# First SwiGLU: the loads of the first wide group's weight sums are put behind the first narrow group's evictions

## The chip, the cores and the metric

The kernel runs on one core of a Trainium2 chip. The metric is the device time of one execution in microseconds (us). The core has five instruction queues that are told of here: PE (TensorE, with PEld for its weight loads), DVE (VectorE), ACT (ScalarE), POOL (GpSimd) and SP (SyncE, which issues DMAs only). DMAs issued by SP appear in the profile as queue q1, those issued by POOL as queue q0.

## The reference, cut to what matters

Two layers, each with a SwiGLU of half weight, a token mixer of three branches, and a second SwiGLU. The sequence has 256 tokens, the model width is 1024, the inner width of a SwiGLU 2816, and all is in float32.

```
def swiglu_ffn(h, w_in, w_out):
    gate, up = jnp.split(h @ w_in, 2, axis=-1)
    return (jax.nn.silu(gate) * up) @ w_out

for l in range(DEPTH):
    x = x + FFN_RESID * swiglu_ffn(rms_norm(x, ffn1_norm[l]), ffn1_w_in[l], ffn1_w_out[l])
    ...                                      # the mixer
    x = x + FFN_RESID * swiglu_ffn(rms_norm(x, ffn2_norm[l]), ffn2_w_in[l], ffn2_w_out[l])
```

## The kernel before, in words

All weights lie in one stream in HBM, cut into chunks of 128 x 1024 float32 (512 KB). A chunk is loaded by SP into one of five `raw` buffers (`load`, line 145). ACT then copies it into `whi` in the matmul's reduced format (line 172), and DVE writes the remainder into `wlo` (line 173); there are four buffers of each. A product of full precision is made of three matmuls, with the high and low parts of the activations and weights (`mm3x`, lines 218 to 220). `units` is the list of chunks in the order of use, `next_sub` hands out the next split chunk, and splits are made three units ahead (`AHEAD`). The split of a unit comes with high priority. The instructions of each engine stand in an order that the framework's scheduler chooses from a simulated timeline, so an instruction whose operands are free can stand earlier in its queue than in the source.

The first product of a SwiGLU, `h @ w_in`, is done in two ways. Seven narrow groups of 256 gate and 256 up columns are done plainly: four chunks each, 48 matmuls, into two PSUM banks (`ps_in`). When a narrow group's fourth chunk is done (c == 3), ACT makes `s`, the SiLU of the gates (line 511), and DVE multiplies it by the up half into `at` (line 513), for each half b of the tokens. These are the evictions of the group; both need `rs_x`, the reciprocal norm of each token, which POOL computes (line 298) from squares that ACT makes of `x` (line 348).

Two wide groups of 512 columns are done with seven products of blocks in place of eight, in the manner of Strassen and Winograd: blocks b11, b12, b21, b22 of the weights, and sums t1 to t4 of them. The sums t1 = b11 + b12 and t3 = b22 + b12 are made by POOL's DMAs in `load_sums`: four plain loads (line 163), and four that add onto what lies there (line 166). t1 goes to tiles named xsum, two for each wide group, and t3 to ysum. t2 and t4 are made by DVE from these and a loaded block (lines 195 and 190). For the first wide group (j = 0) xsum lies in the buffers `vg` and `zt`, and ysum in `xbc`, which holds the transposed input x0 at the very start. For the second (j = 1) xsum lies in a buffer of its own, `big12b`, and ysum again in `xbc`, after the first group's reads.

`_ffn_order` sets the order of the units. In the first SwiGLU of the program, key (0, 0), twelve narrow units (three groups) come first, then those of the first wide group with narrow ones between: b11, two narrow, t1, one narrow, t2, one narrow, t3, one narrow, b22, one narrow, b21, one narrow, t4, one narrow, and then the second wide group in the same way. In the other SwiGLUs the sums of the first wide group are loaded before the SwiGLU begins; in the first, `load_sums(key, 0)` stands behind the first unit.

At the start SP loads, in this order: the transposed input x0 in four parts with the first chunks between them, chunks up to number 3, the input `x` by tokens (1 MB), a table `cs`, and further chunks with the mixer's `row` and `ws` among them.

Of the kernel before, what the change touches and what calls it, by code (L numbers as in the profile page):

```python
# [54 lines left out]
def _ffn_order(key):  # L55

    narrow = [("n", g, c) for g in range(NARROW) for c in range(4)]
    if key == (0, 0):
        lead, gaps = 12, [[2, 1, 1, 1, 1, 1, 1]] * 2
    else:  # L60
        lead, gaps = 4, [[2] * 7, [2, 1, 1, 2, 1, 1, 2]]
    order, narrow = narrow[:lead], narrow[lead:]
    for j in range(WIDE):
        for names, n in zip((("b11", "b12"), ("t1",), ("t2",), ("t3",), ("b22",), ("b21",), ("t4",)), gaps[j]):
            order += [(name, j, c) for name in names for c in range(2)]
            order += narrow[:n]
            narrow = narrow[n:]
    assert not narrow
    return order
# [39 lines left out]
def tile_trunk(ctx, tc, wst, xtok, xT, pos, pcol, prow, wsT, cst, out):  # L109
    nc = tc.nc  # L110
    act, dve, pool, pe = nc.scalar, nc.vector, nc.gpsimd, nc.tensor
# [22 lines left out]
    def source(i):  # L134
        return wst[starts[i] : starts[i] + P * widths[i]].rearrange("(p n) -> p n", p=P)
# [12 lines left out]

    sums = {}

    def load_sums(key, j):

        if j == 0:
            xs = [bp.tile([P, SUB_MAX], F32, name="xsum", tag=t) for t in ("vg", "zt")]
            sums[key, "y"] = bp.tile([P, 2, SUB_MAX], F32, name="ysum", tag="xbc")
        else:
            both = bp.tile([P, 2, SUB_MAX], F32, name="xsum", tag="big12b")
            xs = [both[:, c] for c in range(2)]
        for c in range(2):
            sums[key, "t1", j, c], sums[key, "t3", j, c] = xs[c], sums[key, "y"][:, c]  # L160
        for name, base in (("t1", "b11"), ("t3", "b22")):
            for c in range(2):
                pool.dma_start(out=sums[key, name, j, c], in_=source(chunk_at[key, (base, j, c)]))
        for name in ("t1", "t3"):
            for c in range(2):
                pool.dma_start(out=sums[key, name, j, c], in_=source(chunk_at[key, ("b12", j, c)]), accum_op=ALU.add)
# [37 lines left out]
    def next_sub():  # L204
        i = st["use"]
        prefetch(AHEAD + 1)
        st["use"] += 1
        return splits.pop(i)
# [7 lines left out]
    def mm3x(ps, xhi, xlo, whi, wlo, first, last, again=False):  # L216

        pe.matmul(ps, lhsT=xhi, rhs=whi, start=first, stop=False, skip_group_check=again)  # L218
        pe.matmul(ps, lhsT=xhi, rhs=wlo, start=False, stop=False, skip_group_check=again)  # L219
        pe.matmul(ps, lhsT=xlo, rhs=whi, start=False, stop=last, skip_group_check=again)  # L220
# [89 lines left out]
    def halves(b):  # L310
        return slice(P * b, P * (b + 1))
# [54 lines left out]
    def combined(nrm, n, hi, lo):  # L366

        x11, x21 = nrm.full[:, 0:4, 0:P], nrm.full[:, 0:4, P:]
        x12, x22 = nrm.full[:, 4:8, 0:P], nrm.full[:, 4:8, P:]
        if n == 0:  # L370
            o = x22
            dve.tensor_tensor(o, x22, x21, ALU.subtract)
        elif n == 1:
            o = x21
            dve.tensor_tensor(o, x11, x21, ALU.subtract)
        elif n == 2:
            o = x11
            dve.scalar_tensor_tensor(o, x22, -1.0, x11, ALU.mult, ALU.subtract)
        else:
            o = x12  # L380
            dve.scalar_tensor_tensor(o, x11, -1.0, x12, ALU.mult, ALU.subtract)
        act.copy(hi, o)
        dve.tensor_tensor(lo, o, hi.bitcast(F32), ALU.subtract)
        return hi, lo
# [10 lines left out]
    def ffn(key, nrm, nxt, last, late, aside=None):  # L395
# [14 lines left out]
        def turn_all():  # L410
            while turns:
                turn(*turns.pop(0))
# [18 lines left out]
        xs = {}  # L431
# [13 lines left out]
        def wide_step(kind, j):  # L445
            if kind == "b11":
                wide["A"] = acc.tile([P, 512], F32, name="ps_wa", tag="acc")
                product(wide["A"], plain(0, 0), True)
                wide["m"] = snap("m1", "ss")
            elif kind == "t1":  # L450
                wide["D"] = acc.tile([P, 512], F32, name="ps_wd", tag="acc")
                product(wide["D"], summed(xs[0]), True)
            elif kind == "t2":
                product(wide["A"], summed(xs[2]), False)
                wide["u"] = snap("u2", "xp")
            elif kind == "t3":
                product(wide["A"], summed(xs[1]), False)
                wide["v"] = snap("u3", "xp")
                dve.tensor_tensor(wide["v"], wide["v"], wide["D"], ALU.add)
            elif kind == "b22":  # L460
                product(wide["D"], summed(xs[3]), False)
                dve.tensor_tensor(wide["u"], wide["u"], wide["D"], ALU.add)
            elif kind == "b21":
                e = mxp.tile([P, 512], F32, name="ps_we", tag="mx")
                product(e, plain(1, 0), True)
                dve.tensor_tensor(wide["m"], wide["m"], e, ALU.add)
                gated("a0", wide["m"], 0, wide["u"])
            else:
                product(wide["A"], plain(1, 1), False)
                gated("a1", wide["A"], 1, wide["v"])  # L470
                for n in range(2):
                    s = slice(256 * n, 256 * (n + 1))
                    turns.append((2 * NARROW + 4 * j + 2 * n, [wide["u"][:, s], wide["v"][:, s]]))

        ps = None
        for n, (kind, g, c) in enumerate(_ffn_order(key)):
            if n == 8 and aside:
                aside()
            if kind != "n":
                if kind != "b12" and c == 0:  # L480
                    wide_step(kind, g)
                    if kind == "b22" and g == 0:
                        load_sums(key, 1)
                continue
            if c == 0:
                home, tag = (acc, "acc") if g % 2 == 0 else (mxp, "mx")
                ps = [home.tile([P, 512], F32, name="ps_in", tag=tag) for _ in range(2)]
            hi, lo = next_sub()
            for i in range(2):
                k, w = 2 * c + i, slice(512 * i, 512 * (i + 1))  # L490
                for b in range(2):
                    s = halves(b)
                    mm3x(ps[b], hl[:, k, 0, s], hl[:, k, 1, s], hi[:, w], lo[:, w], k == 0, k == KD - 1)
            if n == 0:
                late()
                nrm.finish()
                if key == (0, 0):
                    load_sums(key, 0)
                big = bp.tile([P, 3, 2, 4, P], F32R, name="xs", tag="big12a")
                spots = [(big[:, m, 0], big[:, m, 1]) for m in range(3)]  # L500
                spots.append([tp.tile([P, 4, P], F32R, name="xs", tag="prob") for _ in range(2)])
            elif n in (1, 2):
                for m in (0, 1) if n == 1 else (2, 3):
                    xs[m] = combined(nrm, m, *spots[m])
            turn_all()
            if c == 3:
                aa = []
                for b in range(2):
                    rcb = nrm.rc[:, b : b + 1]
                    s = tp.tile([P, 256], F32, name="s", tag="s")  # L510
                    act.activation(s, ps[b][:, 0:256], AF.Silu, scale=rcb)
                    a = at[:, g % 2, b]
                    dve.scalar_tensor_tensor(a, ps[b][:, 256:512], rcb, s, ALU.mult, ALU.mult)
                    aa.append(a)
                turns.append((2 * g, aa))
        ahl = [parts[f // 12][:, f % 12] if parts[f // 12] is not None else None for f in range(KF)]

        for h in range(2):
# [588 lines left out]
    def late(first=nrm):  # L1107
        for j in range(KD):
            first.keep(j, x0[:, j])
        for h in range(2):  # L1110
            first.squares(h)

    for l in range(DEPTH):
        params = []

        def aside(l=l, params=params):
            if l == 0:
                tables()
            params.extend(mix_params(l))
# [127 lines left out]
```

## Time and profile before

| | |
|---|---|
| median of three runs | 1264.66 us (1264.11 to 1267.06) |
| the profiled execution | 1265.76 us, span 1264.0 us |
| granted TensorE clock, mean | 0.992 |
| PE, PEld busy | 97%, 81% |
| DVE, ACT, POOL busy | 71%, 59%, 13% |
| HBM read | 253.01 MB, 201 GB/s over the span |

The span is the time from the profile's first to its last instruction, on which all times of the timeline are counted. A row of a timeline holds the start, the duration, the engine, the line of the kernel, the operation, its output and inputs, the count of merged instructions, and in square brackets the idle time before it and what ended that. A row of the chain of waits holds a start, a duration, and what the end waited for in that time. A row of a DMA queue holds packets, MB, and the time of its packets as a share of the 16 DMA engines' time in the window. A row of the stretches holds the window, its length, each engine's busy time and count, the granted clock, the DMA engines' share and GB/s. "x" loaded from in_xT is the transposed input x0.

### The profile page before, as it was taken

What the parts mean: (1) busy time and instruction counts of PE and PEld (TensorE: products, weight loads), DVE (VectorE), ACT (ScalarE), POOL (GpSimd) and SP (SyncE); (2) the same over time, 40 slices, a digit from 0 to 9 for tenths busy, and PEclk for the clock granted to TensorE, in tenths of its full rate; (3) what the DMA queues carried; (4) which work ended last, traced back from release to release, by engine and by line L of the source; (5) the groups of instructions that cost most, each with busy time, mean ns of one, the idle gap of its engine ahead of it and who ended that gap; (6) DMA issues with size and microseconds to landing.
All of it is one profiled execution on the core that took longest, in us unless ns stands there. A gap on an engine that the chain in (4) does not pass through costs nothing.

```text
span 1264.0 us, 16840 instructions
## 1 busy us (share of the span) xinstructions
PE 1221.1 (97%) x6236; PEld 1026.0 (81%) x6236; DVE 903.5 (71%) x1223; ACT 741.2 (59%) x1012; POOL 165.9 (13%) x172
## 2 busy tenths in 40 slices
PE   6899999999999899999999999999999999999998
PEld 4688888989888678778888888898888877778886
DVE  4679755897856777877568885578885566878853
ACT  5667644566576466655466664457467654756642
POOL 2100000731400010000001000054251000100000
PEclk8899999999999999999999999999999999999999
DMA  9976665544844397885549655535376456875662
GB/s 299 323 211 220 217 191 155 163 151 163 270 160 163 131 295 221 267 267 209 190 167 310 225 184 204 193 123 200 105 220 198 149 166 195 255 239 195 216 187 80
DMA packets 71651, 255.17 MB, mean 202 GB/s; under 512 B 8080, under 2 KB 8208, under 8 KB 71440
## 3 DMA queue, kind: packets, MB, share of 16 engines
q1 hardware_dynamic: 61488, 219.40, 51.1%
q0 software_dynamic: 9216, 33.56, 10.7%
q10 hardware_dynamic: 864, 1.13, 0.3%
q8 instruction: 49, 0.80, 0.3%
q14 instruction: 34, 0.28, 0.1%
HBM read 253.01 MB, written 1.05 MB: 201 GB/s over the span
## 4 chain that ended last, share of the span: by engine, by line
PE 83%; DMA 6%; DVE 6%; issue 2%; ACT 2%; POOL 1%; SPq 0%; ACTq 0%; DVEq 0%
PE ps_out L220 8%; PE ps_out L218 7%; PE ps_out L219 7%; PE ps_in L219 7%; PE ps_in L218 7%; PE ps_in L220 7%; DMA raw<-in_w 5%; PE ps_g L219 3%; PE ps_g L218 3%; PE ps_g L220 3%; DVE wlo L173 3%; PE ps_in L214 2%; PE ps_in L212 2%; PE ps_in L213 2%; PE ps_wa L219 2%; PE ps_wa L220 2%
## 5 line engine op out<-in xcount | busy, mean ns | idle before, releaser
L173 DVE TENSOR_TENSOR wlo<-raw,whi 128x1024 fp32r<-128x1024 f32 (+3 forms) x401 | 491.1, 1231 | 231.3 <-ACT whi L172 229.0
L172 ACT CAST whi<-raw 128x1024 fp32r<-128x1024 f32 (+3 forms) x401 | 414.1, 1038 | 320.3 <-PE ps_out L220 136.8
L218 PE MATMUL ps_in<-whi,xg 128*128 128x512 f32 x448 | 165.5, 402 | 16.6 <-ACT whi L172 15.5
L219 PE MATMUL ps_in<-wlo,xg 128*128 128x512 f32 x448 | 178.3, 398 | 2.7 <-DVE wlo L173 2.6
L220 PE MATMUL ps_in<-whi,xg 128*128 128x512 f32 x448 | 176.0, 397 | 0.0
L218 PEld LDWEIGHTS ps_in<-whi,xg 128*128 128x128 f32 x448 | 83.7, 191 | 35.2 <-ACT whi L172 17.2
L219 PEld LDWEIGHTS ps_in<-wlo,xg 128*128 128x128 f32 x448 | 85.6, 191 | 24.0 <-DVE wlo L173 5.8
L220 PEld LDWEIGHTS ps_in<-whi,xg 128*128 128x128 f32 x448 | 85.2, 191 | 17.3
L214 PE MATMUL ps_in<-xg,wlo 128*128 128x256 f32 x336 | 95.6, 286 | 1.5 <-DVE wlo L173 1.5
L213 PE MATMUL ps_in<-xg,whi 128*128 128x256 f32 x336 | 95.5, 286 | 0.0
L212 PE MATMUL ps_in<-xg,whi 128*128 128x256 f32 x336 | 94.5, 287 | 0.3
L219 PE MATMUL ps_g<-wlo,xg 128*128 128x512 f32 x192 | 75.8, 395 | 0.0
L219 PE MATMUL ps_out<-wlo,aa 128*128 128x512 f32 x192 | 75.7, 394 | 0.0
L220 PE MATMUL ps_out<-whi,aa 128*128 128x512 f32 x192 | 75.4, 393 | 0.0
L218 PE MATMUL ps_out<-whi,aa 128*128 128x512 f32 x192 | 75.2, 392 | 0.0
L220 PE MATMUL ps_g<-whi,xg 128*128 128x512 f32 x192 | 75.1, 391 | 0.0
L218 PE MATMUL ps_g<-whi,xg 128*128 128x512 f32 x192 | 72.8, 394 | 0.0
L214 PEld LDWEIGHTS ps_in<-xg,wlo 128*128 128x128 f32 x336 | 64.6, 192 | 1.9 <-DVE wlo L173 1.9
L213 PEld LDWEIGHTS ps_in<-xg,whi 128*128 128x128 f32 x336 | 64.7, 192 | 0.7 <-issue 0.3
L212 PEld LDWEIGHTS ps_in<-xg,whi 128*128 128x128 f32 x336 | 63.8, 192 | 1.2 <-ACT whi L172 1.0
L218 PE MATMUL ps_out<-whi,ab 128*128 128x512 f32 x160 | 62.2, 389 | 0.0
L219 PE MATMUL ps_out<-wlo,ab 128*128 128x512 f32 x160 | 62.2, 389 | 0.0
(322 smaller groups left out, 2414.2 us busy)
## 6 DMA issues: line engine op xcount, KB each, us to landing
raw<-in_w SPq DMA_DIRECT2D x397, 512.0 KB, 4.2
xsum<-in_w POOLq DMA_DIRECT2D x32, 512.0 KB, 7.4
ysum<-in_w POOLq DMA_DIRECT2D x32, 512.0 KB, 8.0
raw<-in_w SPq DMA_DIRECT2D x8, 414.0 KB, 3.1
raw<-in_w SPq DMA_DIRECT2D x6, 384.0 KB, 2.9
raw<-in_w SPq DMA_DIRECT2D x4, 276.0 KB, 2.9
x<-in_xT SPq DMA_DIRECT2D x4, 256.0 KB, 9.3
x<-in_x SPq DMA_DIRECT2D x1, 1024.0 KB, 24.3
```

What stands on the lines that cost most here:

```text
L172: act.copy(hi[:, a:b], r[:, a:b])
L173: dve.tensor_tensor(lo[:, a:b], r[:, a:b], hi[:, a:b].bitcast(F32), ALU.subtract)
L212: pe.matmul(ps, lhsT=whi, rhs=xhl[:, 0], start=first, stop=False)
L213: pe.matmul(ps, lhsT=whi, rhs=xhl[:, 1], start=False, stop=False)
L214: pe.matmul(ps, lhsT=wlo, rhs=xhl[:, 0], start=False, stop=last)
L218: pe.matmul(ps, lhsT=xhi, rhs=whi, start=first, stop=False, skip_group_check=again)
L219: pe.matmul(ps, lhsT=xhi, rhs=wlo, start=False, stop=False, skip_group_check=again)
L220: pe.matmul(ps, lhsT=xlo, rhs=whi, start=False, stop=last, skip_group_check=again)
```

## The change

`load_sums` gets an argument `behind`. Where it is given, POOL first copies one column of it into the first column of each of the four sum tiles of that group, and the plain loads, which write the same tiles, follow the copies. In the first SwiGLU alone the call for the first wide group is moved from behind the first unit to behind the evictions of the first narrow group (n == 3), with the output of the second of these evictions as `behind`. The call for the second wide group, and all calls of other SwiGLUs, stay as they are, without a `behind`.

```
-    def load_sums(key, j):
+    def load_sums(key, j, behind=None):
...
         for c in range(2):
             sums[key, "t1", j, c], sums[key, "t3", j, c] = xs[c], sums[key, "y"][:, c]
+            if behind is not None:
+                for t in (xs[c], sums[key, "y"][:, c]):
+                    pool.tensor_copy(t[:, 0:1], behind)
         for name, base in (("t1", "b11"), ("t3", "b22")):
             for c in range(2):
                 pool.dma_start(out=sums[key, name, j, c], in_=source(chunk_at[key, (base, j, c)]))
...
             if n == 0:
                 late()
                 nrm.finish()
-                if key == (0, 0):
-                    load_sums(key, 0)
...
                 turns.append((2 * g, aa))
+                if n == 3 and key == (0, 0):
+                    load_sums(key, 0, aa[1][:, 0:1])
```

More of the change, by code (lines that the diff above doesn't have):

```diff
@@ L149, in tile_trunk, with load_sums @@
     sums = {}
-    def load_sums(key, j):
+    def load_sums(key, j, behind=None):
         if j == 0:
@@ L160, in load_sums @@
             sums[key, "t1", j, c], sums[key, "t3", j, c] = xs[c], sums[key, "y"][:, c]
+            if behind is not None:
+                for t in (xs[c], sums[key, "y"][:, c]):
+                    pool.tensor_copy(t[:, 0:1], behind)
         for name, base in (("t1", "b11"), ("t3", "b22")):
@@ L496, in ffn @@
                 nrm.finish()
-                if key == (0, 0):
-                    load_sums(key, 0)
                 big = bp.tile([P, 3, 2, 4, P], F32R, name="xs", tag="big12a")
@@ L515, in ffn @@
                 turns.append((2 * g, aa))
+                if n == 3 and key == (0, 0):
+                    load_sums(key, 0, aa[1][:, 0:1])
         ahl = [parts[f // 12][:, f % 12] if parts[f // 12] is not None else None for f in range(KF)]
```

## The prediction

> **What bounds the kernel now.** I read the page first, then the stretches of ten microseconds, then the chain of waits at the start, the DMA queues, and last the timeline of POOL, ACT, DVE and PE around the change.
>
> ```profile
> span 1264.0 us, 16840 instructions
> PE 1221.1 (97%) x6236; PEld 1026.0 (81%) x6236; DVE 903.5 (71%) x1223; ACT 741.2 (59%) x1012; POOL 165.9 (13%) x172
> ```
>
> PE is busy for 97% of the span, so an edit can only gain where PE stands still. The stretches show where that is:
>
> ```profile
> core 0: us, PE busy (x) PEld busy (x) DVE busy (x) ACT busy (x) POOL busy (x), PEclk, DMA share, GB/s
> 10.00:20.00 10.00, 5.04 (x14) 3.15 (x12) 4.23 (x8) 5.59 (x12) 2.71 (x4) 0.83 1.05 292
> 20.00:30.00 10.00, 7.15 (x21) 5.23 (x22) 7.05 (x10) 4.18 (x6) 0.97 (x2) 0.66 1.04 304
> 30.00:40.00 10.00, 4.57 (x12) 2.87 (x11) 5.15 (x22) 7.16 (x15) 4.15 (x5) 0.73 1.03 415
> 40.00:50.00 10.00, 10.00 (x45) 8.12 (x43) 7.05 (x10) 5.81 (x9) 0.00 (x0) 0.93 1.05 310
> ```
>
> From 10 to 40 us PE works 16.8 of 30 us, at a granted clock of 0.66 to 0.83, while the DMA engines are full (share 1.03 to 1.05). From 40 us PE has no gap. The chain names what PE waits for:
>
> ```profile
> 9.41 25.86 DMA raw<-in_w
> 35.35 1.05 ACT whi L172
> 39.35 0.43 PE ps_in L220
> 43.09 0.23 PE ps_in L220
> ```
>
> A weight load issued at 9.41 us lands 25.86 us later, at 35.27, and is unit 4, the first of the second narrow group. The last two rows give PE's pace: 0.43 us a product after a gap, 0.23 when it runs on. What fills the DMA engines meanwhile is POOL's queue (q0) beside SP's (q1). The first two rows are of 0 to 36 us, the third of 36 to 42, the last of 42 to 60:
>
> ```profile
> q0 software_dynamic: 1440, 5.24, 51.8%
> q1 hardware_dynamic: 2047, 5.96, 44.5%
> ...
> q1 hardware_dynamic: 666, 2.43, 101.3%
> ...
> q0 software_dynamic: 283, 1.03, 29.0%
> ```
>
> Up to 36 us more than half of the engines' time goes to the weight sums. POOL's timeline shows which:
>
> ```profile
> 1.39 2.29 POOL L163 DMA_DIRECT2D xsum<-in_w  x4 [0.43 <-issue]
> 7.51 0.88 POOL L166 DMA_DIRECT2D xsum<-in_w  x1 [3.84 <-DMA xsum<-in_w]
> 8.08 0.75 POOL L263 CAST posf<-posi 128x2 f32<-128x2 int32 x1
> 14.46 0.86 POOL L166 DMA_DIRECT2D xsum<-in_w  x1 [1.16 <-DMA xsum<-in_w]
> 19.87 1.09 POOL L163 DMA_DIRECT2D ysum<-in_w  x2 [4.55 <-ACT xgf L330]
> 32.79 0.29 POOL L262 CAST upr<-cs 128x128 fp32r<-128x128 f32 x1 [11.83 <-DMA cs<-in_cst]
> 34.59 0.72 POOL L298 TENSOR_TENSOR rs_x<-ms_x,mhalf 128x2 f32<-128x2 f32 x1 [1.50 <-DVE ang L273]
> 38.11 1.83 POOL L166 DMA_DIRECT2D ysum<-in_w  x2
> ```
>
> The code gives one group only two xsum tiles, and four are loaded at 1.39 us: the second wide group's pair has been pulled forward too, since its buffer is free. So by 36 us ten sum loads ran, six plain (four xsum, two ysum) and four accumulating.
>
> **Prices.** Two accumulating loads took 29.0% of 18 us = 5.2 us of all 16 engines, 2.61 each. The ten took 51.8% of 36 = 18.6; less four at 2.61, six plain ones cost 1.37 each. A weight load on q1: 2.43 MB is 4.6 loads of 0.524 MB in 101.3% of 6 us, 1.31 each.
>
> **The change, removed from the start.** The first group's loads: two plain and two accumulating xsum, two plain ysum, 4 x 1.37 + 2 x 2.61 = 10.7 us of the engines ahead of unit 4's landing, for which the engines were full. That load then lands at 35.27 - 10.7 = 24.6, and PE starts on it near 25.7 instead of 36.45. I expect the second group's four xsum loads to stay early: they have no gate, and POOL has nothing else ready. The rest of the early chain:
>
> ```profile
> 30.67 0.39 PE L220 MATMUL ps_in<-whi,xg 128*128 128x512 f32 x1
> 36.45 1.22 PE L218 MATMUL ps_in<-whi,xg 128*128 128x512 f32 x2 [5.39 <-ACT whi L172]
> 42.14 0.71 PE L218 MATMUL ps_in<-whi,xg 128*128 128x512 f32 x2
> ...
> 30.37 0.63 ACT L348 ACTIVATE xsq<-x 128x512 f32<-128x512 f32 x1 [2.79 <-DMA x<-in_x]
> 36.43 0.82 ACT L511 ACTIVATE s<-ps_in,rs_x 128x256 f32<-128x256 f32 x2
> 40.22 1.03 ACT L172 CAST whi<-raw 128x1024 fp32r<-128x1024 f32 x1
> ...
> 38.12 0.86 DVE L513 SCALAR_TENSOR_TENSOR at<-ps_in,rs_x,s 128x256 f32<-128x256 f32 x2
> ```
>
> Unit 5 (PE 42.14) hangs on another chain: x lands (30.37), ACT squares it, POOL makes rs_x, ACT starts the evictions 6.06 us after the landing and splits unit 5 9.85 us after it, behind them. About 2.0 of the 10.7 us are moved after x lands (10.7 - 8.7), so x lands at 30.37 - 8.7 = 21.7, unit 5 is split at 31.6, and PE begins it at 32.7 with the 1.1 us of one split: 9.4 us earlier than 42.14. This is the tighter chain, and the first term: **-9.4**. If ACT's order lets unit 5 pass the evictions, unit 4 (2.8 us at the fast pace) ends at 28.5, so the bound on that side is -13.6.
>
> **Clock.** A rest of 5.39 us before 36.45 was followed by products at 0.43 us, and unit 5 ran at 0.23. If unit 4 ends at 28.5 and unit 5 starts at 32.7, the clock may drop there: 12 products x 0.20 = 2.4 us lost. I enter 0, since unit 4 itself may run slow (5.2 us, ending at 30.9) and close that rest to 1.8 us; the ends are 0 and +2.4. The Trainium skill (TensorE: Matmul & The Clock Gate, What's actually happening) puts the drop after an idle window of about 3.4 us, which by that rule makes a rest of 1.8 us harmless and one of 4.2 us dear; the 5.39 us rest agrees, and nothing quoted here tests the shorter one.
>
> **What is added.** Four one-column copies on POOL: no such row, the nearest are 0.29 us (128x128) and 0.75 (128x2), so 1.2 to 3 us in all; I take 1.2. They wait for the last eviction, which ends 2.55 us after the first L511 starts: 21.7 + 6.06 + 2.55 = 30.4. Behind the waiting copies POOL holds only the sum loads themselves, and perhaps upr and ws, which the mixer needs much later; rs_x can't be behind them, the eviction needs it. SP's queue isn't touched; its own later loads wait for x and for free buffers, and move forward with both. The copies read `at`, rewritten by group 2 some 20 us later: nothing.
>
> **What is late next.** The eight loads are issued from 31.6 on: 4 x 1.37 + 4 x 2.61 = 15.9 us of engines. At the share that q0 had up to 36 us, 51.8%, they need 30.7 us: the last lands near 62.3. Their readers:
>
> ```profile
> 67.01 2.35 DVE L195 TENSOR_TENSOR xsum<-ysum,raw 128x1024 f32<-128x1024 f32 x2
> 69.28 1.22 DVE L173 TENSOR_TENSOR wlo<-raw,whi 128x1024 fp32r<-128x1024 f32 x1
> 73.25 0.62 PE L218 MATMUL ps_in<-whi,xg 128*128 128x512 f32 x2
> ...
> 54.00:57.00 3.00, 3.00 (x16) 2.43 (x15) 2.37 (x3) 1.80 (x2) 0.00 (x0) 1.00 0.63 201
> 57.00:60.00 3.00, 3.00 (x16) 2.46 (x15) 1.92 (x2) 1.41 (x3) 0.00 (x0) 1.00 0.79 284
> 60.00:64.00 4.00, 4.00 (x19) 3.29 (x18) 2.56 (x3) 2.78 (x5) 0.00 (x0) 1.00 0.73 222
> ```
>
> DVE adds ysum for t2 (two L195) and then splits the unit that PE starts at 73.25. Shifted by 9.4 PE wants that unit at 63.85; before it DVE needs a split (1.22) and the second add (1.18), so ysum must be there by 61.4: the last sum is 0.9 late, with no cushion. The engines' free time agrees: from 54 to 64 us they stood idle for 0.37 x 3 + 0.21 x 3 + 0.27 x 4 = 2.8 us only, so what they deliver by 64 can come at best 2.8 us earlier, at 61.2. Meanwhile SP's queue keeps 44.5% of 30.7 us, 10.4 loads, for the 11.1 units that PE takes at 2.76 us (12 x 0.23): short by less than one, which the five raw buffers of the code cover if some are full. A microsecond of lateness costs PE one. I enter **+1**; the ends are 0 (sums ahead of the rest) and +14 (below).
>
> **Sum.** -9.4 + 1 = -8.4 us. After 64 us nothing stands at a fixed time, so the gain is carried to the end. On the profiled execution's 1265.76 us (span 1264.0, 1.76 around it) that is 1257.4. The median, 1264.66, lies 1.10 lower: 1256.3. A measurement of this kernel tells about 0.3%, 3.8 us, from no change.
>
> **Rivals.** (1) *More comes of it.* The second group's loads go behind the first's on POOL, or ACT passes the evictions: the first term becomes -13.6, less 1 to 2 at t2: about 1252.5. For it: the 25.86 us load; against: those loads were pulled to 1.39 us, and the engines' 2.8 us of free time cap what can come forward. (2) *Given back at t2.* The sums land 5 to 9 us after the 61.4 wanted, DVE stands at L195 with its splits queued behind, the clock drops once (2.4): -9.4 + 7 + 2.4 = 0, about 1264.7. For it: no cushion; against: q0's measured share gives 62.3. (3) *Slower.* q0 gets only the 36.1% that it had from 30 to 36 us:
>
> ```profile
> q1 hardware_dynamic: 568, 1.62, 67.0%
> q0 software_dynamic: 249, 0.88, 36.1%
> ```
>
> then 15.9 / 0.361 = 44 us, the last sum lands at 75.6, 14.2 us late: -9.4 + 14.2 = +4.8, 1269.5. It decides from a landing at 74.6 on (13.2 late: +3.8). Against it: that stretch held the tail of two plain loads, not eight queued ones. Slower issues would be another way there; POOL's issues in the whole run (least, median, most, in ns) say how much that is:
>
> ```profile
> L163 POOL DMA_DIRECT2D xsum<-in_w x16: 543/554/693, 1.4 to 1075.5; - x16
> L166 POOL DMA_DIRECT2D xsum<-in_w x16: 853/880/1254, 7.5 to 1082.7; - x16
> ```
>
> At worst 0.14 and 0.37 us over the median an issue, 2.0 us for eight, not thirteen. The Trainium skill (SBUF — State Buffer, SBUF: two separate sides) warns here: DVE work on the port that it shares with GpSimd can keep a POOL-issued DMA from being described, and these loads would now go out while DVE splits; by its figure, an estimate of 3.1 us in place of 0.62 for a blocked one, the eight would come 20 us late. The rows, many of them issued beside DVE's splits, do not agree with so much.
>
> **Chances.** Forecast (gain 5 to 11 us) 0.60; more 0.15; given back 0.15, of which a fifth still passes 3.8 us; slower 0.10. So faster 0.78, same 0.12, slower 0.10. The range takes the forecast, most of "more" and the near part of "given back": 1250 to 1263; the forecast's own is 1253.5 to 1260.
>
> **What would show it.** Right: POOL issues two xsum loads at 1.4 us and the other eight near 30; unit 4 lands near 24.6, x near 21.7; the PE row now at 42.14 stands near 32.7; from 40 us PE again has no gap; L195 waits for ysum by at most a microsecond or two. Wrong: PE idle at ps_wd or ps_wa behind DVE's L195 for over 3 us, four xsum loads no longer early, or unit 4's start moving by much less than 10.

## The result, and the profile after

The changed kernel takes 1260.53 us in the median of 20 runs, the kernel before 1267.09 us in 20 runs beside them: a ratio of 0.9946 with a 95% interval of 0.9929 to 0.9963. That is 6.8 us less (4.7 to 9.0), against the 8.4 us forecast. Measured again (first experiment) the ratio was 0.9931 (0.9913 to 0.9948), 8.8 us (6.6 to 11.0). The medians of one kernel differ by some 3 us between measurements (1267.09, 1268.81, 1265.85 and 1266.25 us for the kernel before), so each ratio holds only against the kernel before in its own measurement.

The stretches of ten microseconds of the changed kernel, with the columns as before (busy times of PE, PEld, DVE, ACT, POOL; granted clock, DMA share, GB/s):

```profile
10.00:20.00 10.00, 6.16 (x23) 3.82 (x22) 7.50 (x12) 8.20 (x16) 0.88 (x1) 1.00 1.06 312
20.00:30.00 10.00, 5.59 (x21) 3.73 (x20) 7.38 (x19) 7.85 (x18) 2.17 (x3) 0.96 1.02 401
30.00:40.00 10.00, 10.00 (x42) 8.10 (x42) 8.10 (x20) 7.94 (x10) 4.56 (x10) 0.87 0.96 336
40.00:50.00 10.00, 10.00 (x48) 8.24 (x47) 4.11 (x5) 4.29 (x6) 1.73 (x2) 1.00 1.04 277
50.00:60.00 10.00, 7.95 (x33) 5.71 (x32) 4.72 (x6) 4.84 (x8) 0.00 (x0) 0.99 1.03 327
60.00:70.00 10.00, 10.00 (x40) 7.99 (x40) 8.83 (x9) 5.53 (x7) 0.00 (x0) 0.84 0.64 204
```

From 30 us on PE is busy, ten microseconds earlier than before. But a hole that the kernel before did not have stands at 50 to 60 us (7.95 of 10 us), and a drop of the clock behind it (0.84). The timeline of POOL shows that the loads went where they were to go (here and in the other fences, only some rows of a view are shown):

```profile
1.38 1.24 POOL L166 DMA_DIRECT2D xsum<-in_w  x2 [0.43 <-issue]
10.13 0.88 POOL L169 DMA_DIRECT2D xsum<-in_w  x1 [0.68 <-DMA xsum<-in_w]
30.51 0.19 POOL L163 COPY ysum<-at 128x1 f32<-128x1 f32 x1
30.83 0.61 POOL L166 DMA_DIRECT2D xsum<-in_w  x1
42.39 0.87 POOL L169 DMA_DIRECT2D ysum<-in_w  x1 [1.42 <-DMA ysum<-in_w]
```

The second group's pair stays at 1.38 us, the first group's eight loads are issued from 30.83 to 42.39. PE, with units 4 and 5:

```profile
26.98 0.73 PE L221 MATMUL ps_in<-whi,xg 128*128 128x512 f32 x2 [2.91 <-ACT whi L175]
29.21 0.79 PE L222 MATMUL ps_in<-wlo,xg 128*128 128x512 f32 x1 [1.50 <-DVE wlo L176]
33.49 0.71 PE L221 MATMUL ps_in<-whi,xg 128*128 128x512 f32 x2
```

Unit 5 starts at 33.49 in place of 42.14, 8.65 us earlier, and without a rest of PE ahead of it. The hole is read from ACT and DVE:

```profile
45.42 1.05 ACT L175 CAST whi<-raw 128x1024 fp32r<-128x1024 f32 x1 [1.58 <-DMA raw<-in_w]
53.07 1.05 ACT L175 CAST whi<-raw 128x1024 fp32r<-128x1024 f32 x1 [2.78 <-DMA raw<-in_w]
56.87 1.04 ACT L175 CAST whi<-raw 128x1024 fp32r<-128x1024 f32 x1 [2.38 <-DMA raw<-in_w]
59.61 2.00 ACT L175 CAST whi<-xsum 128x1024 fp32r<-128x1024 f32 x2
64.97 1.22 DVE L198 TENSOR_TENSOR xsum<-ysum,raw 128x1024 f32<-128x1024 f32 x1
```

ACT waits for weights. The splits of xsum at 59.61 and the add of ysum at 64.97 have no wait ahead of them: the sums, the last of which landed at 57.26, were in time. While the accumulating loads run (43 to 57 us) the two queues stand like this (packets, MB, share of the engines' time):

```profile
q0 software_dynamic: 503, 1.80, 64.4%
q1 hardware_dynamic: 590, 2.15, 40.3%
```

POOL's queue has 64.4% of the engines' time, and weights land for ACT at 45.42, 53.07 and 56.87 with one between the first two: one every 3.8 us, where PE uses one in 2.76. The accumulating loads landed at 45.85, 49.62, 53.46 and 57.26, the weights at 45.35, 49.16, 52.99 and 56.80: one for one. That is 2.61 + 1.31 = 3.9 us of the engines a pair, by the prediction's prices. The Trainium skill (DMA: Bandwidth & Descriptors, Queues, rings and completion order) has it that each DMA engine takes packets from the queues in turn; the trace agrees (503 packets of one queue, 590 of the other), and adds that a packet of the accumulating queue takes nearly twice as long (64.4% for 503 against 40.3% for 590).

To compare kernels I use when DVE has finished the split of a unit: unit 9 (tenth of the first SwiGLU, before the hole), unit 14 (after it), unit 59 (in the second product, when all sums are done) and unit 463, the last. The kernel before has them at 48.62, 61.62, 149.98 and 1250.43 us; each number below is the difference from these in one profile, minus meaning earlier. Since all are taken from a single profile of the kernel before, e6, whose loads run as in that kernel, shows how far they carry: 0.9 us at unit 9, 1.4 at unit 59, 2.9 at the end.

| kernel | unit 9 | unit 14 | unit 59 | unit 463 | ratio of times (95%) |
|---|---|---|---|---|---|
| the change | -8.7 | -2.5 | -3.9 | -0.6 | 0.9946 (0.9929 to 0.9963) |
| e1, the change again | -8.4 | -2.9 | -6.2 | -8.7 | 0.9931 (0.9913 to 0.9948) |
| e2, both groups late | -16.8 | -16.1 | -11.5 | -13.0 | 0.9900 (0.9879 to 0.9921) |
| e11, e2 again | -16.7 | -15.6 | -10.9 | -9.9 | 0.9926 (0.9907 to 0.9946) |
| e3, spread | -8.0 | -7.9 | -6.9 | -9.1 | 0.9932 (0.9913 to 0.9952) |
| e4, plain second loads | -8.4 | -6.1 | -8.4 | -8.3 | 0.9920 (0.9901 to 0.9939) |
| e5, only the second group late | -7.6 | -7.1 | -3.8 | -4.3 | 0.9969 (0.9954 to 0.9985) |
| e6, no wait | +0.9 | +0.9 | +1.4 | -2.9 | 0.9989 (0.9975 to 1.0003) |
| e7, t3 later | -16.8 | -17.6 | -9.2 | -4.2 | 0.9940 (0.9919 to 0.9961) |
| e8, second group later | -16.8 | -15.9 | -10.5 | -5.2 | 0.9945 (0.9930 to 0.9959) |
| e9, b12 once, POOL adds | -16.7 | -17.5 | -9.7 | -9.2 | 0.9922 (0.9899 to 0.9944) |
| e10, b12 once, DVE adds | -16.8 | -11.6 | -9.2 | -7.9 | 0.9917 (0.9895 to 0.9940) |

In the kernel before the split of unit 14 is made ahead of PE, and in the change only just in time, so that column shows more loss than PE has. Counted by PE's own products, the lead in the first profile falls from 8.7 us to 4.2 across the hole (52 to 66 us), and in e1 from 8.4 to 6.3; from there to unit 59 it stays within half a microsecond. The last column of units differs by up to 8 us between two profiles of one kernel (see the end), so mechanisms are read at units 9 to 59 and sizes from the ratios.

### The profile page after: what moved, and what is told of

Same layout as the page of the kernel before. It is cut to its first block, busy times and chain, and to the rows that moved or that the text cites. A ratio compares the mean times of both kernels' runs of the same rounds, so it can differ in the third digit from the quotient of the medians.

```text
span 1263.4 us, 16844 instructions
## 1 busy us (share of the span) xinstructions
PE 1222.4 (97%) x6236; PEld 1025.8 (81%) x6236; DVE 905.8 (72%) x1223; ACT 741.3 (59%) x1012; POOL 163.9 (13%) x176
## 4 chain that ended last, share of the span: by engine, by line
PE 80%; DVE 7%; DMA 6%; ACT 2%; issue 2%; POOL 2%; SPq 0%; ACTq 0%; DVEq 0%
PE ps_out L223 7%; PE ps_out L221 7%; PE ps_out L222 7%; PE ps_in L222 6%; PE ps_in L223 6%; PE ps_in L221 6%; DMA raw<-in_w 4%; DVE wlo L176 3%; PE ps_g L223 3%; PE ps_g L222 3%; PE ps_g L221 3%; PE ps_in L217 2%; PE ps_in L215 2%; PE ps_in L216 2%; PE ps_wa L222 2%
## 5 line engine op out<-in xcount | busy, mean ns | idle before, releaser
L221 PEld LDWEIGHTS ps_in<-whi,xg 128*128 128x128 f32 x448 | 82.9, 189 | 27.9 <-ACT whi L175 10.5
## 6 DMA issues: line engine op xcount, KB each, us to landing
x<-in_x SPq DMA_DIRECT2D x1, 1024.0 KB, 16.8
```

## The experiments

Theory W says that the loads behind the evictions halve the weight stream. Its rivals are S, late sums, and C, chance.

**e1: the changed kernel once more.** No edit.

> The changed kernel once more, for a second profile beside the first. In the first profile the split of unit 6 (counted with the two halves of unit 0) came 9.1 us earlier than in the kernel before, that of unit 14 only 2.5 us earlier, and the end of the first SwiGLU's weights 3.9 us earlier, of which 0.6 us was left at the end. Theory W (the eight sum loads behind the evictions halve the weight stream, and PE runs out of weights at 50 to 60 us): the second profile shows the same, 2 to 4 us at unit 14 and 3 to 6 us at the end of the SwiGLU. Rival C (what is lost is lost by chance, in drops of PE's clock that differ from run to run): the two profiles differ by over 2 us already in the first 60 us, or the part after 220 us differs by 2 us or more between the two profiles of the same kernel. Both can hold: W for the first 100 us, C for the rest. Time: 4 to 9 us under the kernel before.

Measured: 1258.93 us against 1268.81. Up to unit 14 the two profiles agree within 0.5 us. W's first number holds (2.9 us earlier at unit 14), and the second lies just past its 3 to 6 (6.2). Its 50 to 70 us:

```profile
50.00:60.00 10.00, 8.73 (x36) 6.29 (x36) 5.20 (x6) 5.60 (x8) 0.00 (x0) 1.00 1.05 354
60.00:70.00 10.00, 10.00 (x47) 8.26 (x46) 9.93 (x10) 5.73 (x7) 0.00 (x0) 1.00 0.74 243
```

The hole is there again, but the clock stays at 1.00 behind it where the first profile had 0.84 (0.16 x 10 = 1.6 us). C holds for that, and for the part after 220 us; it does not explain the hole.

**e2: both groups late.** `load_sums(key, 1)` gets a `behind` too, for its xsum alone, from the third narrow group (g == 2):

```
+                if g == 2 and key == (0, 0):
+                    gate[key] = aa[1][:, 0:1]
...
-                        load_sums(key, 1)
+                        load_sums(key, 1, gate.get(key), gated=("t1",))
```

> Also the second wide group's four xsum loads wait, behind the third narrow group's evictions (near 55 us), so nothing of the sums is loaded at the start. Theory W: unit 4 lands near 17 us instead of 25.3, and up to t2 the engines have 8 us less to carry (2 x 1.37 + 2 x 2.61), so the hole at 50 to 60 us goes or shrinks to under 2 us: the end of the first SwiGLU comes 8 to 11 us before the kernel before, 4 to 7 us before the change. Rival S (the first group's sums themselves come too late and hold DVE and PE): they come at the same place behind the evictions, so the time is that of the change within 2 us. Rival C: within 2 us of the change.

Measured: 1254.46 us. Unit 4's weights landed at 17.3 us. Four stretches of it:

```profile
10.00:20.00 10.00, 8.23 (x34) 5.76 (x33) 9.53 (x16) 10.00 (x23) 0.58 (x1) 1.00 1.02 411
50.00:60.00 10.00, 9.12 (x41) 6.80 (x39) 6.88 (x8) 4.58 (x5) 0.71 (x1) 1.00 1.03 352
60.00:70.00 10.00, 10.00 (x44) 8.29 (x45) 9.00 (x9) 7.53 (x10) 2.17 (x4) 1.00 1.05 319
70.00:80.00 10.00, 7.01 (x25) 5.07 (x24) 5.83 (x6) 4.02 (x5) 1.77 (x2) 0.83 1.03 354
```

The hole at 50 to 60 us shrinks to 0.9 us, unit 59 comes 11.5 us earlier (W gave 8 to 11): W, and neither S nor C at the size they gave. The times alone say less: the intervals of e2 and e1 overlap (0.9879 to 0.9921 and 0.9913 to 0.9948). Of the 16.8 us at unit 9 some 5 are given back at 70 to 80 us, where the engines are still full (1.03) and PE waits for weights. S has its place here too, on a smaller scale:

```profile
52.32 1.05 ACT L180 CAST whi<-xsum 128x1024 fp32r<-128x1024 f32 x1 [2.93 <-DMA xsum<-in_w]
```

**e3: spread.** The first group's t1 loads return to the start, its t3 loads wait for the first evictions, and the second group's xsum is gated as in e2.

```
+                if key == (0, 0):
+                    load_sums(key, 0, names=("t1",))
...
-                    load_sums(key, 0, aa[1][:, 0:1])
+                    load_sums(key, 0, aa[1][:, 0:1], ("t3",))
```

> The first group's t1 loads (four) go back to the start, where the second group's stood; only its t3 loads (four) wait for the first narrow group's evictions, and the second group's xsum loads wait for the third narrow group's. Early traffic as in the change, half of it behind the evictions. Theory W: up to unit 10 as in the change (9 us ahead of the kernel before), then no hole at 50 to 60 us, since two accumulating loads instead of four stand against the weights: the end of the first SwiGLU 8 to 10 us before the kernel before, total about 9 us under it. Rival S: t3 comes as in the change, t1 far earlier; if t1 was the late one, the same gain, if t3, none. Rival C: within 2 us of the change.

Measured: 1258.35 us. The hole at 50 to 60 us is gone and the lead is kept through unit 14 (-7.9):

```profile
50.00:60.00 10.00, 10.00 (x48) 8.27 (x47) 7.88 (x9) 6.49 (x9) 3.09 (x4) 1.00 0.75 260
```

This is W's mechanism, short of its sum: at unit 59 it is 6.9 and not 8 to 10, since the second group's eight loads now meet at 59 to 89 us and PE waits 1.15 us at 81.15.

**e4: plain second loads.** The first group's second loads do not accumulate, so an addition is left out.

```
+                op = {} if behind is not None else {"accum_op": ALU.add}
+                pool.dma_start(out=..., in_=source(chunk_at[key, ("b12", j, c)]), **op)
```

> The change, but the first group's four second loads are plain loads of the same bytes in place of accumulating ones, so t1 and t3 hold b12 alone (this leaves out an addition). Bytes and issues are the same. Theory W with the price of accumulating (2.61 us of the engines against 1.37): weight loads land every 2.7 us instead of every 3.8 beside them, PE's hole at 50 to 60 us (2.05 us idle and the slow clock after it) goes: the end of the first SwiGLU 7 to 9 us before the kernel before. Rival B (the bytes or the number of loads count, not the adding): as the change within 1 us.

Measured: 1257.63 us; the stretch where the hole was:

```profile
50.00:60.00 10.00, 10.00 (x48) 8.23 (x47) 6.27 (x7) 6.07 (x9) 0.00 (x0) 1.00 0.65 222
```

The queues at 40 to 50 us (packets, MB, share of the engines' time), first in the change:

```profile
q0 software_dynamic: 354, 1.30, 64.9%
q1 hardware_dynamic: 397, 1.45, 39.2%
```

and then in e4:

```profile
q1 hardware_dynamic: 666, 2.45, 61.2%
q0 software_dynamic: 460, 1.65, 41.3%
```

With the same bytes and issues the hole is gone, and unit 59 comes 8.4 us earlier. Weights land at 43.59, 46.15 and 48.71 us, one in 2.56 where the change had one in 3.8. Rival B falls by this profile: the adding is what costs, by its hold on the engines. The times do not tell the two apart (1257.63 us here, 1258.93 in e1). Of the change's 8.4 to 8.7 us at unit 9, nothing is then given back.

**e5: only the second group late.** The first group's loads as before the change, the second's gated as in e2.

> The kernel before, with the first group's eight loads where they were, and only the second group's four xsum loads put behind the third narrow group's evictions. Theory W (engine time ahead of the weights is what counts, whoever owns it): 8.0 us of the engines leave the start, so unit 4 lands near 27.5 us and unit 6 is split about 7 us earlier than before (8 at most); behind it only two accumulating ysum loads stand against the weights, as before, so the lead is kept: the end of the first SwiGLU 6 to 8 us before the kernel before, total 6 to 8 us under it, as much as the change or more. Rival G (what counts is that the first group's loads wait): no gain, within 2 us of the kernel before.

Measured: 1261.47 against 1265.85 us. Unit 9 comes 7.6 us earlier without any wait of the first group: G falls, W's first half holds. Its second half fails: unit 59 comes only 3.8 us earlier, and the time is 3.9 us less (1.9 to 5.8), where W gave 6 to 8 for both. PE's rest ahead of unit 4, and a later wait at 82.92, in the timeline:

```profile
29.46 1.19 PE L226 MATMUL ps_in<-whi,xg 128*128 128x512 f32 x2 [4.63 <-ACT whi L180]
82.92 0.50 PE L227 MATMUL ps_in<-wlo,xg 128*128 128x512 f32 x1 [1.39 <-DVE wlo L181]
```

The loads went into another tight place, as the stretch with that wait shows (PE busy 8.37 of 10 us, engines at 1.01):

```profile
80.00:90.00 10.00, 8.37 (x30) 6.22 (x29) 6.85 (x8) 3.66 (x5) 0.13 (x1) 0.83 1.01 282
```

**e6: no wait.** The call keeps its new place, without `behind`.

```
-                    load_sums(key, 0, aa[1][:, 0:1])
+                    load_sums(key, 0)
```

> The change without the four copies: the call of load_sums stands behind the first evictions in the source, and nothing waits. POOL's queue then has the order of the kernel before. All theories: the time of the kernel before within 0.3%; a gain here would mean that the place in the source, by way of the scheduler, does the work.

Measured: 1264.15 against 1265.85 us, 0.9989 with 1 inside the interval. POOL issues four xsum loads at the start again, and PE has its old rest:

```profile
1.39 2.29 POOL L166 DMA_DIRECT2D xsum<-in_w  x4 [0.43 <-issue]
...
37.14 1.22 PE L221 MATMUL ps_in<-whi,xg 128*128 128x512 f32 x2 [5.31 <-ACT whi L175]
```

The wait does the work, not the place in the source.

**e7: t3 later.** As e2, with the t3 loads behind the second narrow group's evictions (n == 7).

> As the version with both groups late, but the first group's t3 loads wait for the second narrow group's evictions, so that two accumulating loads at a time stand against the weights for longer instead of four in a row. Theory W: the lead near unit 14 (16.8 us there) is kept to within 1 us, and since the engines are full up to 80 us in both, the end of the first SwiGLU comes within 2 us of that version's (11.5 us before the kernel before). Rival S (the first group's sums are on the edge in that version, ACT waited 2.9 us for an xsum load at 52 us): t3 is later by some 8 us, DVE stands at its adds, and 3 us or more of the gain are lost.

Measured: 1256.86 against 1265.85 us. The lead is kept up to unit 14 (-17.6), as W says, and then S is right:

```profile
62.99 1.23 DVE L203 TENSOR_TENSOR xsum<-ysum,raw 128x1024 f32<-128x1024 f32 x1 [2.94 <-DMA ysum<-in_w]
65.43 0.80 PE L226 MATMUL ps_wa<-whi,xs 128*128 128x512 f32 x1 [3.89 <-ACT whi L180]
```

DVE stands at the add for ysum, PE rests for 3.89 us, and unit 59 is 2.2 us worse than in e2, a little less than the 3 that S gave.

**e8: second group later.** As e2, gated by the fourth narrow group (g == 3).

> As the version with both groups late, but the second group's xsum loads wait for the fourth narrow group's evictions, in POOL's queue behind that group's ysum loads. Theory W: the weights between 50 and 75 us come faster (the two stalls at 74 us, 3.0 us with the slow clock after them, go), but the four loads then run near 75 to 90 us, and t1 of the second group is wanted near 84: what is won before is lost there, end of the first SwiGLU 8 to 12 us before the kernel before. Rival S: t1 comes 5 us or more late, PE stands still for it, and the end is 5 to 8 us before the kernel before.

Measured: 1258.60 against 1265.85 us; unit 59 is 10.5 us earlier, inside what W gave, and ACT waits for the second group's t1 where both theories put the loss. PE's longest rest behind it is for DVE:

```profile
97.70 1.05 ACT L180 CAST whi<-xsum 128x1024 fp32r<-128x1024 f32 x1 [2.72 <-DMA xsum<-in_w]
121.13 0.50 PE L227 MATMUL ps_in<-wlo,xg 128*128 128x512 f32 x1 [1.61 <-DVE wlo L181]
```

Counted by its products, PE gives back 3.8 us between 97 and 123 us; how much of that comes from the late t1 is not shown.

**e9 and e10: b12 loaded once.** In place of the four accumulating loads, b12 is loaded plainly into the buffer of the second group's xsum, and POOL (e9) or DVE (e10) adds it to t1 and t3.

```
+            for name in ("t1", "t3"):
+                for c in range(2):
+                    pool.tensor_tensor(sums[key, name, j, c], sums[key, name, j, c], b12[:, c], ALU.add)
```

> The change, with the first group's accumulating loads replaced: b12 is loaded once, plainly, into the second group's xsum buffer (which keeps that group's loads back until it is read), and POOL adds it to t1 and t3 on chip. Behind the evictions stand six plain loads, 6 x 1.37 = 8.2 us of the engines in place of 15.9, and at the start none. Theory W: as early as the version with both groups late up to unit 14 (16 to 19 us ahead), no hole at 50 to 60 us, the end of the first SwiGLU 12 to 15 us before the kernel before; a POOL add of 128x1024 is not in any trace (128x512: 1.40 us, so 2 to 3 us), four of them are hidden before t1 is wanted. Rival P (POOL's adds are too slow, or slow DVE's splits beside them): t1 or t2 comes late, and the gain is that of the version with both groups late or less.

> The same with the four adds on DVE (1.22 us each, 4.9 us in all, in its queue between the splits). Theory W: as with POOL's adds, less up to 5 us where DVE is the last to come: the end of the first SwiGLU 8 to 14 us before the kernel before. Rival P: better than POOL's adds by over 2 us.

Measured: 1256.25 and 1255.62 against 1266.25 us. The engines are relieved as W says (unit 14 at -17.5 in e9), but the 12 to 15 us at unit 59 that it gave for e9 did not come (-9.7); e10 lies inside its 8 to 14 (-9.2). In e9 the adds are slow, DVE's work beside them as well, and ACT waits for them (timeline of POOL, DVE and ACT):

```profile
46.64 2.89 POOL L175 TENSOR_TENSOR xsum<-xsum,b 128x1024 f32<-128x1024 f32 x1 [14.40 <-DMA b<-in_w]
55.17 3.35 POOL L175 TENSOR_TENSOR ysum<-ysum,b 128x1024 f32<-128x1024 f32 x1
53.06 3.23 DVE L211 TENSOR_TENSOR xsum<-ysum,raw 128x1024 f32<-128x1024 f32 x1
55.24 1.05 ACT L188 CAST whi<-xsum 128x1024 fp32r<-128x1024 f32 x1 [4.15 <-POOL xsum L175]
```

b12 comes last of six loads, the four adds wait for it, and t1 is late by POOL's pace: rival P. In e10 the adds stand in DVE's queue ahead of a split that PE wants, and wait there for b12 (timeline of DVE and PE):

```profile
46.58 1.23 DVE L175 TENSOR_TENSOR xsum<-xsum,b 128x1024 f32<-128x1024 f32 x1 [4.74 <-DMA b<-in_w]
50.13 0.80 PE L235 MATMUL ps_in<-wlo,xg 128*128 128x512 f32 x1 [2.55 <-DVE wlo L189]
```

That costs e10 4 of its 17.6 us, counted by PE's products; it gives back another 4 at 70 to 80 us, where PE is busy for 7.55 of 10 us. e10 is not better than e9 by 2 us, so that part of P fails.

**e11: both groups late, again.** The kernel of e2.

> The version with both groups late once more, beside these two, for a second profile and a time on the same chip: 10 to 13 us under the kernel before, the end of the first SwiGLU 10 to 12.5 us earlier.

Measured: 1257.03 against 1266.25 us, 9.4 us less, and unit 59 10.9 us earlier: the mechanism repeats, the whole time falls short of the 10 us expected. Of the versions tried, e2's kernel has the lowest ratio in its first measurement (1254.46 us beside 1258.93 for the change, in one measurement); in this one it does not differ from e9 and e10. That it beats the change is shown for the first 150 us (by 4.7 us or more between any two profiles), and not by the intervals of the times.

## Why the prediction was right, point by point

- **The loads taken from the start.** Right. Unit 4's weights were to land at 24.6 us and landed at 25.3 (24.9 in e1), x at 21.7 and came at 22.9, PE was to begin unit 4 at 25.7 and did at 26.98. The 10.7 us of engine time, taken from the prices of a plain and an accumulating load, moved the landing by 35.27 - 25.27 = 10.0.
- **The second group's loads stay early.** Right (1.38 us), and worth as much as the first group's: e2 moves them as well, and unit 9 comes another 8 us earlier.
- **The evictions are the tighter chain.** Right in size, but not by that chain: unit 5 at 33.49 against 32.7, 8.65 us earlier where 9.4 was entered. ACT is through with the split of unit 5 at 32.16, behind the evictions as thought:

```profile
31.13 1.03 ACT L175 CAST whi<-raw 128x1024 fp32r<-128x1024 f32 x1
```

PE begins it 1.3 us later, because until then it works on unit 4, whose products stand 0.43 us apart behind the rest of 2.91 us and the wait of 1.50 for DVE. In the kernel before it was the same (split through at 41.25, unit 5 at 42.14, no rest of PE between). So what moved unit 5 is the start of unit 4 (9.47 us earlier), less 0.82 that unit 4 took longer. The two chains lie about a microsecond apart, so the term came out by either; that unit 4 runs slow was weighed under the clock, and entered at 0.
- **What is added.** Right: four copies in under 1 us, the issues from 30.83 (31.6 forecast).
- **The term that was mis-sized: what is late next.** I entered +1 us, for ysum at DVE's add, and held that from 40 us PE again has no gap. The hole is such a gap. The sums came sooner than thought (57.26 against 62.3) and nobody waited for them. What came late were the weights, which the same paragraph had called short by less than one. The error behind both is the share of the two queues: 51.8 and 44.5% were means up to 36 us, over plain and accumulating loads. From 31.6 to 57.3 us they had:

```profile
q0 software_dynamic: 1152, 4.19, 64.0%
q1 hardware_dynamic: 974, 3.54, 37.1%
```

Beside accumulating loads alone a weight landed every 3.8 us, against 2.76 of use, and from 45.42 on, where ACT waits for a load, no full raw buffer was left to cover it. PE gave back 8.65 - 3.9 = 4.8 us in the first profile and 8.4 - 6.2 = 2.2 in e1, where the first has the clock's drop on top. e4 shows the cause: with plain loads it gave back nothing.
- **The rivals.** "Given back at t2" had its price nearly right for the first profile, in the wrong place: at the weights of units 10 to 14, not at t2. "Slower" did not come near; the sums landed 17 us ahead of its point, and POOL's eight issues took 0.53 to 0.90 us each, so none was held up. The 3.1 us that the prediction weighed there was taken over from a case with another operation on DVE, a copy, which it did not say. "More comes of it" needed the second group's loads out of the way, which e2 did; the cap of 2.8 us of free engine time that I set against it is no cap once those loads are moved past it.
- **The cover, and luck.** That the gain at unit 59 is carried to the end holds only roughly: it is 6.2 us there and 8.7 at the end in e1, 3.9 and 0.6 in the first profile. The difference is made in code that the change does not touch, by drops of the clock and by PE's rests. From PE's 500th product on, these take 1.7 and 21.3 us in the kernel before, 3.4 and 22.8 in the first profile, 1.7 and 19.2 in e1. The measured terms give 4 to 6 us, and the measured times 6.8 and 8.8, with intervals that reach down to 4.7 and 6.6. That the time came so near to the 8.4 forecast is in part luck: a first term 0.7 to 1 us too large, a second 1 to 4 us too small, and a rest of the run that differs by several us from profile to profile.

## What to carry to other kernels

Price each transfer in time of the DMA engines, not in bytes, and an accumulating one at about twice a plain one (2.61 against 1.37 us for 512 KB here). When loads are moved out of a full stretch, ask what runs in the stretch that receives them, and compare the pace that is left for the main stream (here one weight in 3.8 us) with the pace at which it is used (2.76), not the mean share with the mean need. Here a prefetch without a gate drifted to the front of its queue (the second group's loads, at 1.39 us), so look there for loads of later stages before moving those of the current one.

## What the runs showed of the hardware that was not expected

The same rest can cost PE its clock or not. In the mixer PE rests for 2.25 us for DVE in every profile; here its timeline and the stretch of 260 to 280 us, first of the kernel before:

```profile
274.69 0.47 PE L684 MATMUL ps_sg<-aseg,upr 128*128 128x512 f32 x1 [2.25 <-DVE aseg L679]
```

```profile
260.00:280.00 20.00, 17.75 (x137) 16.76 (x136) 19.53 (x35) 10.85 (x22) 11.47 (x10) 1.00 0.39 120
```

and then of the changed kernel:

```profile
270.78 0.47 PE L687 MATMUL ps_sg<-aseg,upr 128*128 128x512 f32 x1 [2.25 <-DVE aseg L682]
```

```profile
260.00:280.00 20.00, 17.75 (x125) 16.75 (x124) 19.29 (x27) 10.71 (x22) 11.41 (x9) 0.91 0.34 109
```

With the same rest and the same busy time of PE the granted clock is 1.00 in one and 0.91 in the other, and the changed kernel's lead falls by 1.5 us there. In the eleven other profiles' same stretch it was 1.00 in four and 0.91 or 0.83 in seven. A rest of 2.91 us was followed by slow products at the start too, ahead of unit 4, though there a second one of 1.50 us lies between. The Trainium skill (TensorE: Matmul & The Clock Gate, What's actually happening) has a free-running window of 3.4 us decide, so that where a rest falls in it matters; the traces agree with chance, but not with 3.4 us as the least rest that costs. This is part of the difference from run to run, and one reason why a gain of 4 or 6 us in the first 150 us can read as 0.6 or 8.7 at the end of one profile.

DVE is slowed beside POOL: a DVE add of 128x1024 took 3.23 us beside POOL's adds in e9, where it took 1.22 in the changed kernel (64.97). Whether POOL's own adds (2.40 to 3.36 us) are slowed as well is not shown, since none ran alone. The Trainium skill (SBUF — State Buffer, Who interferes with whom) says that a DVE instruction with two inputs in SBUF contends with a POOL instruction that reads SBUF, and the trace agrees.
